# Five modulation vectors summed beside the FFN's first product, and its first pair of columns computed by eight plain products

## The chip, the cores and the metric

The kernel runs on one core of a Trainium2 chip. The metric is the device time of one execution in microseconds, the median of three runs. The profile is one further execution, recorded by the hardware profiler.

## The reference, cut to what matters

Two transformer blocks run one after the other on one sequence of 1024 tokens with 1024 channels, all in float32. The part that the change touches is the feed-forward network that ends block 1, and the modulation vectors of both blocks:

```python
mod = c_act @ ada_w[i] + ada_b[i]                 # 6 vectors of 1024 (block 1)
sh1, sc1, g1, sh2, sc2, g2 = split(mod, 6)
...
h = rmsnorm(x, ffn_norm_pre) * (1 + sc2) + sh2
a, b = split(h @ ffn_w_in, 2)                     # 1024 x 5632: two halves of 2816 columns
y = (silu(a) * b) @ ffn_w_out                     # 2816 x 1024
x = x + g2 * rmsnorm(y, ffn_norm_post)
...
mod = cond @ mod_w + mod_b                        # block 2: 6 more vectors, from c_2
```

`c` and `c_2` are one row each, so a modulation vector is a row times a 1024 x 1024 matrix: 4 MB are read for 1024 numbers.

## The kernel before

[...] A product is then three matmuls per tile: high x high, high x low, low x high (`mm3` and `product`, lines 214 to 221 and 660 to 668). `split` (lines 161 to 164) makes the parts: ScalarE (ACT) copies to the high part, VectorE (DVE) subtracts.

**The first product.** The transposed activations `T` (1024 channels x 1024 tokens) are cut into four blocks: "00", "10" (the first 512 tokens, channels 0 to 511 and 512 to 1023), and two for the second 512 tokens. The 2816 column pairs are taken in 22 steps of 128 (`NH = 22`), step j with one unit of 128 columns from each half of `ffn_w_in`. A plain way needs 8 block products a step (2 units x 2 channel halves x 2 token halves). The kernel uses a scheme with sums of blocks that needs 7: `block_sums` (lines 590 to 632) forms the sums `t1` to `t4` of the activations and their parts once; `left_sums` (lines 634 to 648) forms the matching sums of the weights for every step. `first_two(j)` computes the two products that need no sum (`a11` x "00" and `a12` x "10"), `pair(j)` the other five; each product is 12 matmuls of 512 columns. `prep(j)` loads the two units of a step (512 KB each, tile `raw`, three buffers) and makes the split and the sums. In the loop over j, `prep(j + 1)` is advanced by one step after each product of `pair(j)`.

Before the loop three steps are begun early (`EARLY = 3`): their upper units are split, and their first two products run while the norm of the residual (`norms`) and the block sums are still being computed, mostly on DVE. `prep(0)` follows the block sums, for its sums are written to `SP`, which takes the place of the activations `Y`. The results go to DRAM (`midh`, `midl`).

**The second product** runs in three passes over the 2816 rows of `ffn_w_out` (units 0 to 7, 8 to 15, 16 to 21), each pass over eight row tiles of 128 tokens. For each row tile `load_mid` loads `mth` and `mtl` back, two row tiles ahead.

**The modulation vectors** `G2`, `A3`, `B3`, `Gm`, `A4`, `B4`, `Ge` are computed by `mod_steps` (lines 239 to 270) beside passes 0 and 1: for each vector eight loads of 512 KB into `raw` and eight DVE operations (lines 250 and 252) that add a block of 128 matrix rows, scaled by `cc`, to `acc`; then matmuls with ones sum over the partitions (line 256), DVE adds the bias and the gain from `quad` tiles, and a store writes the vector to DRAM. `mods` is advanced five steps after each row tile.

**The order of the work.** The source issues everything in one sequence, with generators advanced at chosen places. A planner in the kernel framework then fixes the order on each engine and queue at build time: source order is the priority, and an instruction goes ahead of an earlier one where its operands and buffers are there first by the planner's own costs. Buffers of one tag (`raw` 3, `wh` 3, `wl` 3, `k2` 4, `h2` 8, `k4` 8) are handed out as they come free. All loads and stores of this part go through SyncE's queue (SP). Products take PSUM buffers by `pany`, alternating between two sets of three.

Of the kernel before, what the change touches and what calls it, by code (L numbers as in the profile page):

```python
# [10 lines left out]
F32 = mybir.dt.float32  # L11
F32R = mybir.dt.float32r
I32 = mybir.dt.int32
AF = mybir.ActivationFunctionType
OP = mybir.AluOpType
# [4 lines left out]
D = 1024  # L20
# [15 lines left out]
class Kernel:  # L36
# [199 lines left out]
        for g in groups:  # L236
            yield from self.mod_steps(*g)

    def mod_steps(self, m, cc, vectors):


        nc, a = self.nc, self.a
        w, b = a[m + "_w" + self.suffix[m]], a[m + "_b" + self.suffix[m]]
        for name, j, g in vectors:
            acc = self.k4([128, D], "acc")
            for k in range(8):
                raw = self.wp.tile([128, 1024], F32, name="raw", bufs=self.raw_bufs)
                nc.sync.dma_start(raw, w[0, k * 128:(k + 1) * 128, j * D:(j + 1) * D])
                if k == 0:
                    nc.vector.tensor_scalar(acc, raw, cc[:, 0:1], None, op0=OP.mult)  # L250
                else:
                    nc.vector.scalar_tensor_tensor(acc, raw, cc[:, k:k + 1], acc, op0=OP.mult, op1=OP.add)  # L252
                yield
            ps = self.pany()
            for q in range(4):
                nc.tensor.matmul(ps[32 * q:32 * q + 32, 0:256], self.one[:, 0:32], acc[:, q * 256:(q + 1) * 256],
                                 start=True, stop=True, tile_position=(0, 32 * q))

            def quad(v):
                t = self.k2([128, 256], "quad")  # L260
                nc.sync.dma_start(t, bass.AP(tensor=v.tensor, offset=v.offset, ap=[[256, 4], [0, 32], [1, 256]]))
                return t

            t = self.k2([128, 256], "quad")
            nc.vector.tensor_tensor(t, ps[:, 0:256], quad(b[0, j * D:(j + 1) * D]), op=OP.add)
            if g is not None:
                nc.vector.scalar_tensor_tensor(t, t, g[0], quad(a[g[1]]), op0=OP.add, op1=OP.mult)
            d = self.r[name] = self.dram.tile([1, D], F32, name="r" + name)
            nc.sync.dma_start(d.rearrange("o (q n) -> (o q) n", q=4), t[0:128:32, :])
# [400 lines left out]
    def block1_ffn(self, dbg=None):  # L670
        nc, tc, a = self.nc, self.tc, self.a
        V = nc.vector
        TH, TL, Y = self.TH, self.TL, self.Y
        w_in, w_out = a["ffn_w_in"], a["ffn_w_out"]
        NH = 22
# [18 lines left out]
        src = lambda j: [w_in[0, :, c:c + 128].rearrange("(k p) m -> p k m", p=128) for c in (j * 128, (NH + j) * 128)]  # L694
        W, TT = {}, {}

        def upper(j, raw):
            W[j] = [self.wp.tile([128, 1024], F32R, name=n, bufs=self.hl_bufs) for n in ("wh", "wl")]
            self.split(W[j][0], W[j][1], raw)

        def prep(j, lone):

            raw = [self.raw_unit(u, (8, 128)) for u in src(j)]
            if not lone:
                upper(j, raw[0])
            yield
            W[j] += [self.k2([128, 512], n, F32R) for n in ("a22h", "a22l")] + [SP[:, j % 2 * 4 + n] for n in range(4)]
            yield from self.left_sums(raw, W[j][2:4], W[j][4:])

        def first_two(j):  # L710

            A, T = self.left_parts(W[j]), self.T
            TT[j] = t = {}
            ps = self.pany()
            self.product(ps, A["a11"], T["00"])
            t[0] = self.h2([128, 512], "p1")
            nc.scalar.activation(t[0], ps, AF.Copy)
            yield
            ps = self.pany()
            self.product(ps, A["a12"], T["10"])  # L720
            t[2] = self.h2([128, 512], "sa")
            V.tensor_tensor(t[2], ps, t[0], op=OP.add)
            nc.scalar.activation(t[2], t[2], AF.Silu)

        def out(j, half, m):
            s = slice(half * 512, half * 512 + 512)
            h, l = self.h2([128, 512], "mh", F32R), self.h2([128, 512], "ml", F32R)
            self.split(h, l, m)
            for d, t in zip(midd, (h, l)):
                nc.sync.dma_start(d[j, :, s], f32(t))  # L730
# [29 lines left out]
            out(j, 1, t[3])  # L760
            del W[j], TT[j]

        EARLY = 3
        for j in range(EARLY):
            upper(j, self.raw_unit(src(j)[0], (8, 128)))
        self.T = {"00": ([TH[:, k, 0:512] for k in range(4)], [TL[:, k, 0:512] for k in range(4)]),
                  "10": ([TH[:, 4 + k, 0:512] for k in range(4)], [TL[:, 4 + k, 0:512] for k in range(4)])}
        early = [first_two(j) for j in range(EARLY)]
        for _ in norms:
            next(early[0], None)  # L770
        for f in early[:2]:
            for _ in f:
                pass
        for k, _ in enumerate(self.block_sums(B2)):
            if k == 1:
                for _ in early[2]:
                    pass
        SP = self.region(1, "SP", F32R)
        for _ in prep(0, True):
            pass  # L780
        for j in range(NH):
            nxt = prep(j + 1, j + 1 < EARLY) if j + 1 < NH else iter(())
            for _ in pair(j, j < EARLY):
                next(nxt, None)
            for _ in nxt:
                pass


        cc2 = self.silu_col(a["c_2"], "cc2")
        mods = self.all_mods(("ada", self.cc, (("G2", 5, (0.0, "ffn_norm_post")),)),  # L790
                             ("mod", cc2, (("A3", 1, (1.0, "norm1_g_2")), ("B3", 0, None), ("Gm", 2, None),
                                           ("A4", 4, (1.0, "norm2_g_2")), ("B4", 3, None), ("Ge", 5, None))))
        wide = lambda f: [f([128, 1024], n, F32R) for n in ("oh", "ol")]
        wpt = lambda: [self.wp.tile([128, 1024], F32R, name=n, bufs=self.hl_bufs) for n in ("wh", "wl")]
        U = {}
# [24 lines left out]
        for at, (c, i) in enumerate(todo):  # L820
            last = c == 2
            if (c, i) == (1, 6):
                for _ in mods:
                    pass
            if (c, i) == (1, 7):
                G2, A3 = self.bcast(self.r["G2"], "G2"), self.bcast(self.r["A3"], "A3")
                B3 = self.load_cols(self.const, self.r["B3"], "B3")
                self.cw = self.load_cols(self.const, a["conv_w_2"], "cw", 32)
                self.cbias = self.load_cols(self.const, a["conv_b_2"], "cvb", 8)
            mt = mts.pop((c, i))  # L830
            pss = [self.pany(), self.pany()]

            order = passes[c] if c else [0, 1, 2, 3, 4, 5, 6, 7]
            for n, j in enumerate(order):
                u = j - passes[c][0]
                for nh in range(2):
                    q = slice(nh * 512, nh * 512 + 512)
                    h, l = U[j][0][:, q], U[j][1][:, q]
                    nc.tensor.matmul(pss[nh], mt[0][:, u], h, start=n == 0, stop=False)
                    nc.tensor.matmul(pss[nh], mt[0][:, u], l, start=False, stop=False)  # L840
                    nc.tensor.matmul(pss[nh], mt[1][:, u], h, start=False, stop=n == len(order) - 1)
            for nh in range(2):
                q = slice(nh * 512, nh * 512 + 512)
                if c == 0:
                    nc.scalar.activation(Y[:, i, q], pss[nh], AF.Copy)
                else:
                    V.tensor_tensor(Y[:, i, q], Y[:, i, q], pss[nh], op=OP.add)
            if at + 2 < len(todo):
                load_mid(*todo[at + 2])

            if c == 0 and i in (3, 4, 5):
                unit(8 + i - 3, (OH[:, 5 + i - 3], OL[:, 5 + i - 3]))
            if c == 0 and i == 7:
                for j in range(11, 16):
                    unit(j, (OH[:, j - 11], OL[:, j - 11]))
            if c == 1 and i < 6:
                unit(16 + i, wpt() if i < 3 else wide(self.k4))
            if c < 2:
                for _ in range(5):
                    next(mods, None)  # L860
            else:
                if i == 0:
                    TH, TL = self.TH, self.TL = self.region(2, "TH", F32R), self.region(3, "TL", F32R)
                    norms = self.norms(lambda i: self.residual_norm(
                        i, G2, A3, x1[rows(i), :], self.x2[rows(i), :], self.xt_slot(i, True)))
                next(norms)
                if i == 6:
                    self.half_to_T(0, B3)
# [1073 lines left out]
```

## Time and profile before

| | |
|---|---|
| timed runs | 2839.19, 2839.96, 2842.51 us; median 2839.96 |
| profiled execution | 2849.81 us, span 2848.1 us from first to last instruction |
| busy over the span | PE 92%, weight loads 74%, DVE 62%, ACT 44%, POOL 8% |
| moved by DMA | 443 MB, mean 156 GB/s |

The profile's page names engines as PE (TensorE matmuls), PEld (weight loads), DVE, ACT, POOL and SP, and lines as L252. A share of busy time over the whole span averages stages with different limits, so the stretches around the change are read one by one: the start of the first product (about 485 to 513 us), its loop (513 to 922 us), passes 0 and 1 of the second product (922 to 1144 us).

### The profile page before, as it was taken

Reading aid. Unit: us, or ns where it says so; the run is one execution under the profiler, and the core shown is the slowest. Engines: PE = TensorE matmul, PEld = TensorE weight load, DVE = VectorE, ACT = ScalarE, POOL = GpSimd, SP = SyncE. Lnnn points to the kernel's source line nnn. Section 1 sums busy time; section 2 is a strip of 40 time slices with the busy share of each in tenths; the row PEclk is TensorE's granted clock in tenths of the full one; section 3 lists DMA queues with packets and bytes.
Section 4 is the critical chain, followed back from the end, with each engine's and each line's share of the span. In section 5 each row is a group of like instructions: output and inputs, shape, how many; then the busy total and the mean of one; then the engine's idle time right before and its main releaser. Section 6 shows DMA issues by size and latency. Waiting matters only on the chain. (4 is left out here: it accounts for less than half of the span.)

```text
span 2848.1 us, 36415 instructions
## 1 busy us (share of the span) xinstructions
PE 2631.1 (92%) x13146; PEld 2117.0 (74%) x13146; DVE 1777.7 (62%) x3672; ACT 1252.6 (44%) x2184; POOL 215.2 (8%) x204
## 2 busy tenths in 40 slices
PE   6999997899999989899999999999999999798882
PEld 4766675688887767778988888788887878677772
DVE  6666549877676454676510444547777468788885
ACT  4666645333333110144321333334555444677782
POOL 0000011000000000100000000000000200333320
PEclk9999999899999999999999999999999999899996
DMA  7233122332334887434434554551111454799995
GB/s 242 89 97 97 36 89 97 118 119 96 111 118 155 275 272 245 133 115 151 139 111 103 181 163 142 176 189 39 30 31 40 155 199 146 249 331 327 311 327 181
DMA packets 318828, 443.17 MB, mean 156 GB/s; under 512 B 41665, under 2 KB 215806, under 8 KB 318646
## 3 DMA queue, kind: packets, MB, share of 16 engines
q1 hardware_dynamic: 309430, 424.02, 45.2%
q0 software_dynamic: 9216, 16.81, 2.5%
q8 instruction: 104, 1.70, 0.3%
q14 instruction: 78, 0.64, 0.1%
HBM read 355.44 MB, written 102.06 MB: 161 GB/s over the span
## 5 line engine op out<-in xcount | busy, mean ns | idle before, releaser
L164 DVE TENSOR_TENSOR wl<-raw,wh 128x1024 fp32r<-128x1024 f32 (+3 forms) x106 | 130.7, 1233 | 246.7 <-ACT wh L163 236.2
L163 ACT ACTIVATE wh<-raw 128x1024 fp32r<-128x1024 f32 (+3 forms) x106 | 110.4, 1043 | 277.9 <-PE pss L220 134.6
L164 DVE TENSOR_TENSOR mgl<-X,MH 128x1024 fp32r<-128x1024 f32 x91 | 110.1, 1221 | 16.0 <-ACT MH L163 15.4
L252 DVE SCALAR_TENSOR_TENSOR acc<-raw,cc,acc 128x1024 f32<-128x1024 f32 x70 | 89.8, 1283 | 43.1 <-DMA raw<-in_mod_w_dram 35.8
L163 ACT ACTIVATE MH<-X 128x1024 fp32r<-128x1024 f32 x91 | 96.2, 1060 | 38.1 <-DMA X<-in_w_expert_up_dram 16.5
L1744 PEld LDWEIGHTS pss<-mgl,xh 128*128 128x128 f32 x512 | 96.4, 188 | 22.1
L221 PE MATMUL pss<-TH,wl 128*128 128x512 f32 x280 | 111.4, 398 | 0.0
L219 PE MATMUL pss<-TH,wh 128*128 128x512 f32 x280 | 111.1, 397 | 0.0
L220 PE MATMUL pss<-TL,wh 128*128 128x512 f32 x280 | 110.9, 396 | 0.0
L1744 PE MATMUL pss<-mgl,xh 128*128 128x256 f32 x512 | 102.6, 281 | 0.0
L1742 PE MATMUL pss<-MH,xh 128*128 128x512 f32 x256 | 102.5, 400 | 0.0
L1745 PE MATMUL pss<-MH,xl 128*128 128x512 f32 x256 | 101.0, 394 | 0.0
L440 DVE CUSTOM_DVE_ANT_0 pp<-pss,bias 128x384 f32<-128x384 f32 (+1 forms) x128 | 63.4, 521 | 54.4 <-PE pss L436 53.5
L549 POOL TENSOR_TENSOR Y<-Y,G 128x1024 f32<-128x1024 f32 x16 | 39.5, 2467 | 743.5 <-DMA xt<-in_x_dram 412.7
L219 PE MATMUL mm<-TH,wh 128*128 128x512 f32 x232 | 93.1, 401 | 2.4 <-ACT TH L175 1.3
L220 PE MATMUL mm<-TL,wh 128*128 128x512 f32 x232 | 92.3, 398 | 0.0
L221 PE MATMUL mm<-TH,wl 128*128 128x512 f32 x232 | 92.3, 398 | 0.0
L228 PE MATMUL mm<-TH,wh 128*128 128x512 f32 x192 | 78.0, 407 | 1.6 <-ACT TH L348 1.6
L447 ACT ACTIVATE pp<-pp,mx 128x384 f32<-128x384 f32 (+1 forms) x128 | 73.8, 579 | 11.6 <-DVE mx L443 11.6
L219 PE MATMUL mm<-WD,mTh 128*128 128x512 f32 x128 | 55.3, 432 | 24.9 <-ACT mTh L163 24.8
L229 PE MATMUL mm<-TL,wh 128*128 128x512 f32 x192 | 77.5, 404 | 0.6 <-DVE TL L349 0.6
L230 PE MATMUL mm<-TH,wl 128*128 128x512 f32 x192 | 76.6, 399 | 0.0
(732 smaller groups left out, 8154.7 us busy)
## 6 DMA issues: line engine op xcount, KB each, us to landing
raw<-in_mod_w_dram SPq DMA_DIRECT2D x48, 512.0 KB
raw<-in_ffn_w_in_dram SPq DMA_DIRECT2D x47, 512.0 KB
X<-in_w_expert_gate_dram SPq DMA_DIRECT2D x47, 512.0 KB
X<-in_w_expert_down_dram SPq DMA_DIRECT2D x47, 512.0 KB
X<-in_w_expert_up_dram SPq DMA_DIRECT2D x44, 512.0 KB
raw<-in_w_in_dram SPq DMA_DIRECT2D x40, 512.0 KB
raw<-in_ada_w_dram SPq DMA_DIRECT2D x32, 512.0 KB
midh<-mh SPq DMA_DIRECT2D x44, 256.0 KB
```

Of the source, the lines that this page charges most:

```text
L163: self.nc.scalar.activation(h, src, AF.Copy)
L164: (engine or self.nc.vector).tensor_tensor(l, src, f32(h), op=OP.subtract)
L219: nc.tensor.matmul(ps, ah, bh, start=i == 0, stop=False)
L220: nc.tensor.matmul(ps, ah, bl, start=False, stop=False)
L221: nc.tensor.matmul(ps, al, bh, start=False, stop=i == n - 1)
L228: nc.tensor.matmul(ps, ah, bh, start=i == 0, stop=False)
L229: nc.tensor.matmul(ps, ah, bl, start=False, stop=False)
L230: nc.tensor.matmul(ps, al, bh, start=False, stop=i == n - 1)
L252: nc.vector.scalar_tensor_tensor(acc, raw, cc[:, k:k + 1], acc, op0=OP.mult, op1=OP.add)
L1742: nc.tensor.matmul(ps, xh[:, k], gh, start=k == 0, stop=False)
L1744: nc.tensor.matmul(ps[:, c], xh[:, k], self.ML[n + c][:, m], start=False, stop=False)
L1745: nc.tensor.matmul(ps, xl[:, k], gh, start=False, stop=k == 7)
```

## The change

Five of the seven vectors (`G2`, `A3`, `B3`, `Gm`, `A4`) are advanced inside the loop over pairs, three steps in each pair from j = 2 on; `B4` and `Ge` stay beside passes 0 and 1, now two steps after each row tile. `late=3` puts three empty steps between a vector's last DVE operation and its matmuls. For the five, `acc` takes a buffer of the tag `wl` instead of `k4`. The start of the first product: step 0 is computed by eight plain products, four (`usual_first`) beside the norms and four (`usual_second`) after the block sums; only step 1 is begun early by its first two products, and the loop starts at j = 1.

```diff
-    def mod_steps(self, m, cc, vectors):
+    def mod_steps(self, m, cc, vectors, late=0, wl=False):
...
-            acc = self.k4([128, D], "acc")
+            acc = self.wp.tile([128, D], F32, name="acc", tag="wl", bufs=self.hl_bufs) if wl else self.k4([128, D], "acc")
...
+                yield
+            for _ in range(late):
                 yield
             ps = self.pany()
...
-        EARLY = 3
-        for j in range(EARLY):
-            upper(j, self.raw_unit(src(j)[0], (8, 128)))
+        C = []
+        for u in src(0):
+            C += [self.wp.tile([128, 1024], F32R, name=n, bufs=self.hl_bufs) for n in ("wh", "wl")]
+            self.split(C[-2], C[-1], self.raw_unit(u, (8, 128)))
+        upper(1, self.raw_unit(src(1)[0], (8, 128)))
...
-        early = [first_two(j) for j in range(EARLY)]
+        parts = [self.left_parts(C[0:2]), self.left_parts(C[2:4])]
+        kept = []
+
+        def usual_first():
+            for n, A in enumerate(parts):
+                ps = self.pany()
+                self.product(ps, A["a11"], self.T["00"])
+                p = self.h2([128, 512], "p1")
+                nc.scalar.activation(p, ps, AF.Copy)
+                yield
+                ps = self.pany()
+                self.product(ps, A["a12"], self.T["10"])
+                t = self.h2([128, 512], "c1")
+                V.tensor_tensor(t, ps, p, op=OP.add)
+                kept.extend((p, t))
+                if n == 0:
+                    nc.scalar.activation(t, t, AF.Silu)
+                    yield
+            V.tensor_tensor(t, t, kept[1], op=OP.mult)
+            out(0, 0, t)
+
+        def usual_second():
+            for A, p in zip(parts, (kept[0], kept[2])):
+                ps = self.pany()
+                self.mm3(ps, [(A[x][0][k], A[x][1][k], self.T[y][0][k], self.T[y][1][k])
+                              for x, y in (("a11", "t1"), ("a12", "11")) for k in range(4)])
+                V.tensor_tensor(p, ps, p, op=OP.add)
+                if p is kept[0]:
+                    nc.scalar.activation(p, p, AF.Silu)
+            V.tensor_tensor(p, p, kept[0], op=OP.mult)
+            out(0, 1, p)
+
+        f = usual_first()
         for _ in norms:
-            next(early[0], None)
-        for f in early[:2]:
-            for _ in f:
-                pass
+            next(f, None)
+        for _ in f:
+            pass
+        f = first_two(1)
         for k, _ in enumerate(self.block_sums(B2)):
-            if k == 1:
-                for _ in early[2]:
-                    pass
+            next(f, None)
+        usual_second()
         SP = self.region(1, "SP", F32R)
-        for _ in prep(0, True):
+        for _ in prep(1, True):
             pass
-        for j in range(NH):
-            nxt = prep(j + 1, j + 1 < EARLY) if j + 1 < NH else iter(())
-            for _ in pair(j, j < EARLY):
+        cc2 = self.silu_col(a["c_2"], "cc2")
+        mods = self.all_mods(("ada", self.cc, (("G2", 5, (0.0, "ffn_norm_post")),), 3, True),
+                             ("mod", cc2, (("A3", 1, (1.0, "norm1_g_2")), ("B3", 0, None), ("Gm", 2, None),
+                                           ("A4", 4, (1.0, "norm2_g_2"))), 3, True))
+        for j in range(1, NH):
+            nxt = prep(j + 1, False) if j + 1 < NH else iter(())
+            for n, _ in enumerate(pair(j, j == 1)):
                 next(nxt, None)
+                if j > 1 and n in (0, 2, 4):
+                    next(mods, None)
             for _ in nxt:
                 pass
-        cc2 = self.silu_col(a["c_2"], "cc2")
-        mods = self.all_mods(...)
+        for _ in mods:
+            pass
+        mods = self.all_mods(("mod", cc2, (("B4", 3, None), ("Ge", 5, None)), 3))
...
             if c < 2:
-                for _ in range(5):
+                for _ in range(2):
                     next(mods, None)
```

## Rows read from the trace of the kernel before

**Rows 1.** The page's 40 slices, tenths: granted clock of PE, share of DMA.
```profile
PEclk9999999899999999999999999999999999899996
DMA  7233122332334887434434554551111454799995
```

**Rows 2.** Busy time by stretch; counts in brackets, then granted clock, DMA share, GB/s.
```profile
485.00:513.00 28.00, 10.87 (x53) 8.20 (x52) 25.53 (x39) 14.16 (x23) 0.00 (x0) 0.70 0.07 21
...
620.00:776.00 156.00, 156.00 (x675) 126.42 (x674) 110.67 (x152) 54.64 (x72) 0.00 (x0) 1.00 0.33 109
922.00:1144.00 222.00, 195.22 (x829) 149.72 (x829) 106.27 (x108) 30.66 (x39) 0.00 (x0) 0.94 0.83 260
```

**Rows 3.** Timeline of one pair in the loop: start, duration, engine, line, operation.
```profile
598.21 0.38 SPq L189 DMA_DIRECT2D raw<-in_ffn_w_in_dram  x1
...
602.31 1.06 ACT L163 ACTIVATE wh<-raw 128x1024 fp32r<-128x1024 f32 x1 [2.86 <-PE pss L668]
...
607.64 0.63 ACT L163 ACTIVATE a22h<-raw 128x512 fp32r<-128x512 f32 x1 [4.27 <-PE pss L667]
...
616.43 1.23 DVE L164 TENSOR_TENSOR SP<-raw,SP 128x1024 fp32r<-128x1024 f32 x1 [0.40 <-ACT SP L163]
...
617.68 0.39 SPq L189 DMA_DIRECT2D raw<-in_ffn_w_in_dram  x1
...
635.50 0.40 PE L666 MATMUL mm<-t2h,SP 128*128 128x512 f32 x1
```

**Rows 4.** Waits of PE, 922 to 1144 us: total, times, longest.
```profile
PE mm L256 <- DVE acc L252: 11.1, 3, 4.8
PE pss L256 <- DVE acc L252: 8.6, 1, 8.6
...
PE pss L839 <- DMA mth<-midh: 2.0, 1, 2.0
```

**Rows 5.** Timeline of PE behind the longest of these waits.
```profile
1059.50 0.63 PE L840 MATMUL pss<-OL,mth 128*128 128x512 f32 x1
...
1062.84 0.39 PE L840 MATMUL pss<-OL,mth 128*128 128x512 f32 x1
```

**Rows 6.** Busy time by stretch, start of the second product.
```profile
920.00:930.00 10.00, 8.35 (x36) 6.02 (x34) 6.72 (x9) 4.69 (x7) 0.34 (x1) 1.00 1.02 305
930.00:940.00 10.00, 8.84 (x31) 6.91 (x32) 4.49 (x4) 2.11 (x2) 0.00 (x0) 0.83 0.84 276
```

**Rows 7.** Timeline of PE: a vector's eight matmuls beside the attention.
```profile
165.61 0.64 PE L256 MATMUL mm<-acc,one 128*32 128x256 f32 x8
```

**Rows 8.** The page's costliest groups: busy us, mean ns, idle before and releaser.
```profile
L252 DVE SCALAR_TENSOR_TENSOR acc<-raw,cc,acc 128x1024 f32<-128x1024 f32 x70 | 89.8, 1283 | 43.1 <-DMA raw<-in_mod_w_dram 35.8
```

**Rows 9.** Waits of DVE in the loop, 620 to 776 us.
```profile
DVE p L741 <- PE pss L668: 10.1, 12, 1.4
...
DVE u L741 <- PE pss L668: 8.2, 4, 2.1
DVE wl L164 <- ACT wh L163: 4.3, 8, 0.8
DVE SP L164 <- ACT SP L163: 3.2, 8, 0.4
```

**Rows 10.** Timeline of the stop at the start of the first product.
```profile
503.57 0.75 DVE L630 SCALAR_TENSOR_TENSOR TL<-pss,B,TH 128x512 fp32r<-128x512 f32 x1
...
508.17 0.80 PE L666 MATMUL mm<-TH,SP 128*128 128x512 f32 x1 [13.43 <-ACT SP L163]
...
512.71 0.39 PE L666 MATMUL pss<-t2h,SP 128*128 128x512 f32 x1
```

**Rows 11.** Waits of DVE on loads, 922 to 1144 us.
```profile
DVE acc L252 <- DMA raw<-in_mod_w_dram: 35.8, 26, 5.0
...
DVE acc L252 <- DMA raw<-in_ada_w_dram: 6.8, 4, 2.9
```

More of the change, by code (lines that the diff above doesn't have):

```diff
@@ L784, in block1_ffn @@
                 next(nxt, None)
+                if j > 1 and n in (0, 2, 4):
+                    next(mods, None)
             for _ in nxt:
                 pass
-        cc2 = self.silu_col(a["c_2"], "cc2")
-        mods = self.all_mods(("ada", self.cc, (("G2", 5, (0.0, "ffn_norm_post")),)),
-                             ("mod", cc2, (("A3", 1, (1.0, "norm1_g_2")), ("B3", 0, None), ("Gm", 2, None),
-                                           ("A4", 4, (1.0, "norm2_g_2")), ("B4", 3, None), ("Ge", 5, None))))
+        for _ in mods:
+            pass
```

## The prediction

> **What bounds the kernel now.** I read the 40 slices first: where DMA stands at nine tenths while PEclk dips, TensorE waits for transfers; where both are calm it computes [rows 1]. The second view, busy time by stretch, splits the part around the change into three stages [rows 2]. In the loop over column pairs (620 to 776 us) PE is busy without a gap at full clock, 156.00 of 156.00 us, VectorE (DVE) is busy 110.67 us and the DMA share is 0.33: TensorE bounds it. In passes 0 and 1 of the second product (922 to 1144 us) PE is busy 195.22 of 222.00 us, the clock is 0.94 and the DMA share 0.83. At the start of the first product (485 to 513 us) PE is busy 10.87 of 28.00 us and DVE 25.53: DVE bounds it.
>
> The pitch of a 512-column product comes from the loop: a load of `raw` is issued 19.47 us after its like of the pair before [rows 3], and a pair has 7 products of 12 matmuls, so 19.47 / 84 = 0.232 us, or 2.78 us a product. Passes 0 and 1 hold 2 passes x 8 row tiles x 8 units x 2 halves x 3 = 768 matmuls, 178.0 us. They took 222, so 44 us are lost there. [...] The start of the stage costs 4.5 us: 36 + 31 matmuls in 20 us where 86 would fit [rows 6]. That start waits for units of `ffn_w_out`, not for vectors, and stays.
>
> **The change, part by part.**
>
> *Passes 0 and 1 lose five of seven vectors.* Forty loads of 512 KB go, 21.0 MB of the 260 GB/s x 222 us = 57.7 MB [rows 2]. What is left, 36.7 MB, asks for some 196 GB/s over 187 us, three quarters of what the stage carries now. The two vectors left get two steps per row tile instead of five and their PE part comes three steps after the last sum, 1.5 row tiles or 16 us later; the longest wait for a sum was 8.6 us [rows 4]. So I count all four waits and the slow clock behind them as gone. After: 178.0 for the products, 2 x 0.64 = 1.3 for the vectors' own matmuls (eight in 0.64 us [rows 7]), 4.5 for the start, and something for waits that remain on `mth`, `mtl` and units. That last term lies between 0 (nothing late) and what today's loss leaves: 44.0 - 7 x 0.64 for seven vectors' matmuls - 4.5 for the start - 19.7 = 15.3 us, which is the clock lost behind the four waits and the waits on transfers. Of the second sort the row shows 2.0 us on `mth` [rows 4]; I take 3.5, near it, with something for the clock, since row tile 7 of pass 0 still asks for five units at once. Sum 187.3, a gain of 34.7 us; its bounds are 38.2 and 22.9.
>
> *The pair loop gets them.* PE: 5 x 0.64 = +3.2 us, for PE has no gap there to hide it. DVE: 40 operations on `acc` of 1.283 us [rows 8], 51 us, and eight short ones on a quarter of the columns, 0.32 each by an estimate from that width: 54 us, less a little because the first of each vector has one operand fewer; 52 over the 18.3 pairs that 55 steps need at three a pair, 2.84 us a pair. DVE now works 110.67 / 8 = 13.83 us a pair [rows 2] and waits 36.0 us in eight pairs for PE itself (four rows, from 10.1 to 8.2 [rows 9]), 4.5 a pair. The addition fits into the wait for PE and leaves 1.66 us a pair. It hides because evictions may lag: six PSUM buffers at 2.78 us a product. If that cover were gone, all 52 us would show. SP: 40 loads, 5 + 3 rows of bias and gain, 5 stores and one row of `c_2` at some 0.38 us of issue each [rows 3] are 21 us on a queue that issues six transfers a pair. Behind them in that queue stand the next pair's loads and the stores of `mh`/`ml`; POOL's queue is untouched.
>
> *Buffers.* A pair's two loads hold two of the three `raw` buffers; forty vector loads pass through what is free, 2.2 a pair. Vector data taken late delays the next pair's left sums. Those have room: issued at 598.21, split from 607.64, done by 617.7, first used at 635.50 [rows 3], some 18 us of slack. `acc` now takes one of three `wl` buffers, so upper weights can be split only one pair ahead, which is all that PE needs. The five `quad` tails take slots that `a22h`/`a22l` use and can hold them for two loads and a store, 12 us at most if each takes the 4.1 us from a load's issue to its first use (598.21 to 602.31 [rows 3]): inside the 18 us, and if it were not, PE would wait for the excess, five times. For all of this I take +1 us, with 0 below and rival C on the other side. The row of `c_2` and its transpose are put ahead of the loop: 0 to 3 us, counted in that 1.
>
> *The first pair by eight products.* Before the stop PE has six products in either version (3 x 2 before, 4 + 2 after). The stop: PE waits 13.43 us for `SP`, to 508.17, and then runs at the lower level until 512.7 [rows 10]. After it stand 3 x 5 + 19 x 7 = 148 products before, and 4 + 5 + 20 x 7 = 149 after. But the first four of those, 11.1 us, need only `t1` and `11`, whose last low part is written at 503.57 to 504.3 [rows 10], so they run inside the stop, and 145 stand behind it: 3 x 2.78 = 8.3 us less. Against that, DVE, the bound here, gets one multiplication and one low part more ahead of the block sums and four such operations beside the left sums, each some 0.75 as line 630 [rows 10], so `SP` comes 1.5 to 4.5 us later. The clock lost after the stop (508.17 to 512.71 at half pace, 2.3 us) is partly saved. I take a gain of 6 us; bounds 10 (all in the stop, most of the clock kept) and -2.8 (nothing hidden, one product more).
>
> *Sum.* -34.7 + 3.2 + 1 - 6 = -36.5 us. The profiled execution is 2849.8 us (span 2848.1 and 1.7 around it), so 2813.3 by its own time. The three timed runs have a median of 2840.0, 0.35% lower; the same difference gives 2803.5, rounded 2804.
>
> **Rivals.**
>
> B. The second product stays bound by its own transfers. For it: share 0.83 now, and rows show waits on `mth` and units that are no vector's. Against: 196 GB/s is asked where 260 is carried. Then all of the 15.3 us stays: -22.9 + 4.2 - 6 = -24.7, 2815. Its cost above that would be loads that come later than today, for which no row speaks.
>
> C, on the other side: DVE becomes the bound of the pair loop. Its order is fixed when the kernel is built; a sum whose load is late holds back every eviction and left sum behind it. Place: pairs 2 to 19. Point: 1.66 us a pair, 30 us over 18 pairs, is 0.75 us for each of 40 loads; beyond that each microsecond of mean wait costs 40, and at 1.66 us the whole gain is eaten. In the second product the sums waited 42.6 us in 30 cases, 1.42 each, 0.76 over all 56 loads, the longest 5.0 [rows 11]. With half the longest, 2.5: 40 x 1.75 = +70, 2873. Against: that was at a DMA share of 0.83; here it goes from 0.33 (109 GB/s) to some 0.5 by 60 GB/s more, and 42.6 of the 43.1 us that this line was idle in the whole kernel [rows 8] lie in the second product: next to none beside the attention, where three vectors are summed through the same three buffers.
> [...]
>
> D. The eight-product start gains nothing: one product more and the added DVE work shift everything, +2.8 instead of -6: 2813. For it: DVE is busy 25.53 of 28 us there. Against: the four products need no left sums.
>
> E. The change doesn't do what it says: the planner leaves the vectors' loads behind the pairs' own until the loop ends, and the drain there costs what the stage saved: about 2838. Against: three steps a pair stand in the source order, and buffers come free twice a pair.
>
> **Chances.** Forecast 0.60, B 0.15, C 0.10, D 0.10, E 0.05. The likeliest case alone lies in 2795 to 2813 (-38.2 + 3.2 - 10 = -45; -31 + 4.2 + 0 = -26.8). For 8 in 10 I take 2791 to 2833: the forecast's own range with 4 us below (the timed runs differ by 3.3), B, D and the mild end of C (mean wait 1.42 us: +27, 2831); E and most of C lie outside. A measurement here tells 0.2%, 5.7 us, from no change. Faster by more: forecast, B, D, 0.85. Within: E, 0.05. Slower: C, 0.10.
>
> **What would show it.** In the profile after: PE without a gap through the pair loop, DVE near 16.7 us a pair, DMA share near 0.5; passes 0 and 1 in 184 to 191 us with no wait of line 256 on line 252; PE busy between 495 and 508 with `TH`/`wl` products of the first pair. DVE above 19 us a pair including waits on `raw`, or PE waiting for `SP` inside the loop, shows C. `mth` waits above 7 us show B. A stop before the first `SP` product of more than 5 us shows D. The prediction is wrong above all if loads inside the loop come later than the left sums' 18 us of slack.

## The result, and the profile after

The kernel after takes 2808.64 us (median of four runs, 2806.95 to 2810.86) against 2841.24 for the kernel before (median of four, the three known before among them): ratio 0.9884, 95% interval 0.9867 to 0.9901, or 32.6 us faster. The forecast was 2804 in 2791 to 2833. The profiled execution, one of these four, took 2807.7 us where the sum said 2813.3.

Busy time by stretch of the kernel after; columns as in [rows 2]:
```profile
485.00:513.00 28.00, 22.25 (x97) 17.10 (x96) 27.82 (x43) 15.98 (x26) 0.00 (x0) 0.88 0.02 6
620.00:776.00 156.00, 156.00 (x684) 125.37 (x683) 131.64 (x174) 53.51 (x72) 0.00 (x0) 1.00 0.54 173
918.00:1103.60 185.60, 182.30 (x787) 145.72 (x788) 55.13 (x60) 30.52 (x38) 0.00 (x0) 0.99 0.62 193
```
Beside [rows 2], PE is busy for twice as long at the start; in the loop it still has no gap, while DVE's busy time rises from 110.67 to 131.64 us, 16.5 a pair; passes 0 and 1 take 185.6 us where they took 222, at a DMA share of 0.62 instead of 0.83.

All waits of PE in passes 0 and 1 after (total, times, longest):
```profile
PE pss L880 <- ACT OH L163: 3.4, 2, 2.2
```
The waits for sums of [rows 4] are gone, and the one row left is the start of the stage. Line 880 is the old 839; 668 to 670 are the old 666 to 668, 743 and 753 evictions (VectorE takes a finished product out of its PSUM buffer), 258 the old 256.

PE at the start of the first product, after:
```profile
490.84 0.77 PE L609 MATMUL pt<-ident,Y 128*128 128x128 f32 x4 [2.37 <-ACT x L621]
...
501.62 0.79 PE L219 MATMUL pss<-TH,wh 128*128 128x512 f32 x1 [3.37 <-ACT TH L163]
...
510.61 0.50 PE L668 MATMUL mm<-TH,SP 128*128 128x512 f32 x1
```
The wait of 13.43 us for `SP` [rows 10] has become one of 3.37 us for a part of `t1`; from there the plain products of step 0 run, and `SP` is no longer waited for.

DVE in the loop, 530 to 900 us, the waits that stand before or in a sum's chain:
```profile
DVE acc L252 <- DMA raw<-in_mod_w_dram: 17.8, 18, 2.2
DVE wl L164 <- ACT wh L163: 7.9, 9, 2.5
...
DVE acc L252 <- DMA raw<-in_ada_w_dram: 1.7, 4, 0.6
...
DVE acc L250 <- DMA raw<-in_ada_w_dram: 0.9, 1, 0.9
```
Sums do wait for their loads, 20.4 us over 40 loads, 0.51 each, and PE doesn't notice.

To compare kernels by stage I use three starts of every trace: the first matmul of the second half of the attention's output projection (about 401 us), the first of pass 0 and the first of pass 2. Lengths in us, worked out from these starts (a second profile of before and of after are the runs e0 and a1):

| kernel | to pass 0 | passes 0, 1 | timed median, ratio to before |
|---|---|---|---|
| before / e0 | 521.56 / 521.56 | 220.96 / 219.73 | |
| after / a1 | 518.36 / 518.68 | 184.51 / 184.39 | 2808.64, 0.9884 / 2806.06, 0.9867 |
| e1 start alone | 514.17 | 216.50 | 2835.74, 0.9977 |
| e2 vectors alone | 525.26 | 184.61 | 2813.55, 0.9900 |
| e3 empty steps alone | 521.70 | 206.16 | 2832.58, 0.9963 |
| e4 seven vectors, four steps | 528.83 | 181.90 | 2819.20, 0.9916 |
| e5 more DVE work | 518.31 | 184.63 | 2807.08, 0.9872 |
| e8 four steps | 526.45 | 184.13 | 2811.86, 0.9892 |
| e9 no empty steps | 524.75 | 182.44 | 2815.59, 0.9895 |
| e6 order of pass 0 | 517.09 | 183.03 | 2805.61, 0.9868 |
| e7 norm on DVE | 507.48 | 184.78 | 2792.87, 0.9823 |
| e10 both | 506.01 | 182.83 | 2790.97, 0.9819 |

The median of before lay between 2843.39 and 2844.64 us in the comparisons with e1 to e10.

### The profile page after: what moved, and what is told of

Its sections match the earlier page's. It is cut to its first block, busy times and chain, and to the rows that moved or that the text cites. A ratio compares the mean times of both kernels' runs of the same rounds, so it can differ in the third digit from the quotient of the medians.

```text
span 2805.8 us, 36372 instructions
## 1 busy us (share of the span) xinstructions
PE 2627.1 (94%) x13158; PEld 2116.6 (75%) x13158; DVE 1765.9 (63%) x3663; ACT 1249.7 (45%) x2183; POOL 219.3 (8%) x204
## 5 line engine op out<-in xcount | busy, mean ns | idle before, releaser
L164 DVE TENSOR_TENSOR wl<-raw,wh 128x1024 fp32r<-128x1024 f32 (+2 forms) x107 | 132.9, 1242 | 243.7 <-ACT wh L163 233.0
L163 ACT ACTIVATE wh<-raw 128x1024 fp32r<-128x1024 f32 (+2 forms) x107 | 111.5, 1043 | 238.2 <-PE mm L220 142.1
L164 DVE TENSOR_TENSOR mgl<-X,MH 128x1024 fp32r<-128x1024 f32 x91 | 110.0, 1221 | 16.5 <-ACT MH L163 16.0
L221 PE MATMUL mm<-TH,wl 128*128 128x512 f32 x288 | 114.6, 398 | 0.0
L219 PE MATMUL mm<-TH,wh 128*128 128x512 f32 x288 | 114.5, 397 | 0.0
L220 PE MATMUL mm<-TL,wh 128*128 128x512 f32 x288 | 114.2, 396 | 0.0
L163 ACT ACTIVATE MH<-X 128x1024 fp32r<-128x1024 f32 x91 | 96.3, 1062 | 37.8 <-DMA X<-in_w_expert_up_dram 15.9
L219 PE MATMUL pss<-TH,wh 128*128 128x512 f32 x240 | 97.8, 408 | 5.7 <-ACT TH L163 4.4
L220 PE MATMUL pss<-TL,wh 128*128 128x512 f32 x240 | 96.6, 403 | 0.0
L221 PE MATMUL pss<-TH,wl 128*128 128x512 f32 x240 | 96.3, 401 | 0.0
L228 PE MATMUL mm<-TH,wh 128*128 128x512 f32 x192 | 78.5, 410 | 1.0 <-ACT TH L350 1.0
L229 PE MATMUL mm<-TL,wh 128*128 128x512 f32 x192 | 77.6, 404 | 0.0
L230 PE MATMUL mm<-TH,wl 128*128 128x512 f32 x192 | 76.6, 399 | 0.0
```

What stands on the lines that cost most here:

```text
L163: self.nc.scalar.activation(h, src, AF.Copy)
L164: (engine or self.nc.vector).tensor_tensor(l, src, f32(h), op=OP.subtract)
L219: nc.tensor.matmul(ps, ah, bh, start=i == 0, stop=False)
L220: nc.tensor.matmul(ps, ah, bl, start=False, stop=False)
L221: nc.tensor.matmul(ps, al, bh, start=False, stop=i == n - 1)
L228: nc.tensor.matmul(ps, ah, bh, start=i == 0, stop=False)
```

## The experiments

**The two parts apart, e1 and e2.**
```diff
 # e1: kernel after, vectors as in the kernel before
-        mods = self.all_mods(("ada", self.cc, (...), 3, True), ("mod", cc2, (...), 3, True))
...
-                if j > 1 and n in (0, 2, 4):
-                    next(mods, None)
...
+        mods = <all seven, behind the loop, five steps a row tile>
 # e2: kernel before, with the lines that e1 takes out added and EARLY = 3 kept
```


> The eight-product start of step 0 alone; all seven vectors stay beside passes 0 and 1, five steps a row tile, no empty steps. Theory T1 (the gain is the sum of two independent parts: passes 0 and 1 relieved of five vectors, and the start's stop filled with four products): the start alone gives 6 to 8 us over the kernel before, 2833 to 2835, and PE's waits for the vectors' sums (line 252) in passes 0 and 1 stay near the 19.7 us of the kernel before. Rival R1 (the start only moves the wait, DVE being the bound there): within 2 us of before. Rival R2 (the start gives all that the forecast missed and more): 10 us or more.

> The five vectors moved beside the first product with their empty steps, but the three early steps of the kernel before at the start. T1: 26 to 31 us faster than before, 2810 to 2815; passes 0 and 1 in 184 to 188 us and the loop longer by 3 to 4 us. Rival R2: 20 us or less. If the two parts need each other (the start leaves fewer upper units in the buffers that the sums now share), this one is slower than T1 says by the waits on wl buffers in the first pairs: 5 to 10 us.

e1: ratio 0.9977 (0.9968 to 0.9986), by the ratio 6.5 us. e2: 0.9900 (0.9883 to 0.9916), 28.4 us. Together 34.9, against 32.6 measured for both at once: within the intervals the parts are independent, as T1 says, and R1, R2 and the coupling through `wl` fall. The stages show more than the times: the start alone shortens the way to pass 0 by 7.4 us, the vectors lengthen it by 3.70 (e2 against before) or 4.19 (after against e1), and passes 0 and 1 take 184.6 us with the vectors' move alone. In e1, whose profiled execution lies at its timed median (2835.37 against 2835.74), these passes take 216.5 us with all seven vectors in them. Measured from there the move gives 31.9 us and costs 3.7, 28.2 in all, as e2's time says; measured from the profile of before it would be 36.4 - 3.7 = 32.7.

Waits of PE in passes 0 and 1 of e1:
```profile
PE pss L258 <- DVE acc L252: 10.3, 3, 4.4
PE mm L258 <- DVE acc L252: 9.7, 3, 8.1
```
20.0 us of waits for sums, as in [rows 4]. The stop of e2, which keeps the old start:
```profile
502.89 0.24 PE L133 MATMUL pt<-ident,crow 8*128 8x8 f32 x1 [8.68 <-DMA crow<-in_c_dram]
507.64 0.80 PE L668 MATMUL mm<-TH,SP 128*128 128x512 f32 x1 [4.52 <-ACT SP L163]
```
The transpose of `c_2`'s row is queued inside the stop and costs nothing there: 8.68 + 4.52 are 13.2 us, and before waited 13.43.

**The empty steps alone, e3.**
```diff
 # kernel before
-        ("ada", self.cc, (("G2", ...),)), ("mod", cc2, (...))
+        ("ada", self.cc, (("G2", ...),), 3), ("mod", cc2, (...), 3)
...
-                for _ in range(5):
+                for _ in range(6):
```


> All seven vectors stay beside passes 0 and 1 and only PE's part of each is put three steps later (six steps a row tile, so that the loads keep about their pace). Rival R3 (PE's waits for the sums are the loss, so the empty steps alone recover it): the 19.7 us of waits and the slow clock behind them go, 20 to 28 us faster than before. T1 (the transfers of 58 MB in this stage are the loss; a wait for a sum is where it shows): 12 us faster at most, with the DMA share still above 0.8 and waits of PE on mth, mtl or units in the place of those on sums.

Ratio 0.9963 (0.9950 to 0.9976), 10.5 us. R3 falls: putting PE's part later recovers 10.5 of the 28.4 us that e2's move gives, and part of that may come from the loads, which run at 4.4 a row tile here (6 steps, 8 loads in 11) instead of 5. Waits of PE in e3, 900 to 1145 us (its line 841 is the old 839), and the first wait of DVE, 922.8 to 1129 us:
```profile
PE mm L258 <- DVE acc L252: 5.7, 2, 3.6
PE mm L841 <- DMA mth<-midh: 3.3, 1, 3.3
PE pss L258 <- DVE acc L252: 3.0, 3, 1.5
```
```profile
DVE acc L252 <- DMA raw<-in_mod_w_dram: 32.2, 23, 3.5
```
8.7 us of waits for sums remain, a wait of 3.3 us on `mth` stands beside them (2.0 in [rows 4]), and the sums themselves still wait for their loads, at a DMA share of 0.86 in this stage: late loads are behind the loss, and a later place for PE's part only moves where that is felt. Whether the rate of the transfers or their issue through three `raw` buffers makes them late, no run tells apart: in the kernel before the queue stands 34.9 us until a sum frees a buffer for the next vector load (922 to 1144 us).

**What VectorE bears in the loop, e5.**
```diff
                     nc.vector.scalar_tensor_tensor(acc, raw, cc[:, k:k + 1], acc, op0=OP.mult, op1=OP.add)
+                if wl:
+                    nc.vector.tensor_tensor(raw, raw, raw, op=OP.max)
```


> The kernel after with one more VectorE operation behind each of the 40 additions of a vector in the loop (the maximum of a raw tile with itself, in place, 128 x 1024; 1.22 us like line 164 of that shape; the tile's buffer is held that much longer). 40 x 1.22 = 49 us over 18.3 pairs, 2.7 us a pair: DVE 16.5 + 2.7 = 19.2 of a 19.47 us pair, and with the mean wait for raw (0.51 us x 2.2 loads a pair = 1.1) 20.3. Theory C1 (in the loop VectorE's busy time and its waits for raw add up against the pair, and only the excess shows): 0.8 us x 18 pairs, some 15 us slower than after, 2820 to 2828, with stops of PE on evictions. Rival C2 (the waits are swallowed by the slack of the evictions): within 3 us of after. Rival C3 (any delay of VectorE shows in full): 45 us or more slower.

2807.08 us, ratio 0.9872 (0.9856 to 0.9888), and 518.31 us to pass 0 against 518.36: nothing. C1 and C3 fall. Busy time of e5 in the loop, and two of its DVE waits, 530 to 900 us:
```profile
620.00:776.00 156.00, 156.00 (x685) 125.29 (x684) 148.29 (x191) 53.48 (x72) 0.00 (x0) 1.00 0.52 168
```
```profile
DVE acc L252 <- DMA raw<-in_mod_w_dram: 2.5, 6, 0.9
...
DVE wl L164 <- ACT wh L163: 2.1, 2, 1.3
```
DVE is busy 148.29 of 156 us, 95%, and PE has no gap. The waits for `raw` fell from 20.4 to 3.6 us (2.5 + 0.7 + 0.4): the added operations run where DVE had stood waiting. Busy time and waits don't add up, so the 1.66 us a pair of the prediction was no limit.

**The pace of the loads, e4, e8 and e9.**
```diff
 # e4: all seven vectors in the loop; e8: the five of the change; both:
-                if j > 1 and n in (0, 2, 4):
+                if j > 1 and n in (0, 1, 2, 4):
 # e9: kernel after
-        (..., 3, True) ... (..., 3)
+        (..., 0, True) ... (..., 0)
```


> The kernel after with all seven vectors beside the first product, four steps a pair in place of three; nothing is left beside passes 0 and 1. T1: the loop pays 2 x 0.64 = 1.3 us more of PE, DVE goes from 16.5 to some 17.4 us of a 19.5 us pair and still hides; passes 0 and 1 lose the 1.3 us of PE that move: the same time as the kernel after within 2 us, 2807 to 2811. Rival C (DVE with its late loads is near the bound of the loop): the 56 sums wait more, pairs stretch past 19.6 us, 8 us or more slower than after.

> The kernel after, its five vectors at four steps a pair in place of three: the same 40 loads and sums, done in 14 pairs instead of 18. It tells whether the 8 us that seven vectors at four steps lost come from the pace (theory C1: 2.9 sums a pair, a stop of PE inside the loop of 6 us as there, some 5 to 10 us slower than after) or from the two vectors more and their work at the loop's end (rival: within 2 us of after, no stop of PE inside the loop).

> The kernel after without the three empty steps, in the loop and in passes 0 and 1: PE's eight matmuls of a vector follow its last sum in the source order, as in the kernel before. Theory D1 (sums in the loop are seldom late, so the move itself is nearly the whole gain and the empty steps only insure it): within 3 us of after, with PE's waits for line 252 below 3 us in total. Rival D2 (the move needs the empty steps: in the loop PE has no gap, so each of five vectors stops it for the sum's own 1.28 us and the lateness of its load, up to 3 us, and the clock drops behind it): 10 to 20 us slower than after.

e4: ratio 0.9916 (0.9902 to 0.9930), 2819.20 us, some 10 slower than after: rival C's outcome. e8: 0.9892 (0.9875 to 0.9908); its time can't be told from that of after, but the way to pass 0 is 8.1 us longer, most of e4's 10.5. So the two vectors more are not the reason. PE and then DVE at the stop of e8:
```profile
701.67 0.39 PE L670 MATMUL pss<-TH,SP 128*128 128x512 f32 x1
707.35 0.80 PE L668 MATMUL mm<-TH,wh 128*128 128x512 f32 x1 [5.29 <-DVE c L753]
707.94 0.63 PE L669 MATMUL mm<-TL,wh 128*128 128x512 f32 x1
```
```profile
700.16 1.29 DVE L252 SCALAR_TENSOR_TENSOR acc<-raw,cc,acc 128x1024 f32<-128x1024 f32 x1 [1.87 <-DMA raw<-in_mod_w_dram]
701.36 0.68 DVE L743 TENSOR_TENSOR u<-mm,p 128x512 f32<-128x512 f32 x1
702.66 1.22 DVE L164 TENSOR_TENSOR wl<-raw,wh 128x1024 fp32r<-128x1024 f32 x1 [0.62 <-ACT wh L163]
703.81 0.68 DVE L743 TENSOR_TENSOR p<-pss,p 128x512 f32<-128x512 f32 x1
705.41 1.28 DVE L252 SCALAR_TENSOR_TENSOR acc<-raw,cc,acc 128x1024 f32<-128x1024 f32 x1 [0.92 <-DMA raw<-in_mod_w_dram]
706.61 0.69 DVE L753 TENSOR_TENSOR c<-mm,p 128x512 f32<-128x512 f32 x1
```
This is the mechanism of rival C, of which the rows of before held no case. The eviction `c` stands in DVE's queue behind two sums that wait 1.87 and 0.92 us for their loads and a low part that waits 0.62 us for its split. PE waits 5.29 us until `c`, which reads an `mm` buffer, has run; then its matmuls take 0.63 us instead of 0.39 to 0.40. Between 620 and 776 us, the stretch of this stop, DVE was *less* busy than in e5:
```profile
620.00:776.00 156.00, 150.71 (x653) 120.00 (x652) 127.54 (x169) 51.07 (x69) 0.00 (x0) 0.98 0.56 177
```
Nor do the sums of e8 wait longer: 15.9 us from 530 to 900 us (12.4 + 2.8 + 0.7), where the kernel after has 20.4. What counts is what stands behind a late sum. And it is one stop: e8 has no other in its 14 pairs at this pace, and e4 loses 6.13 us at the same place of the same order (308.4 us after the start that all traces share, e8 306.6) and 0.58 at one other.

e9 was meant to test the empty steps as cover for PE's part. It missed that question: PE never waits for line 252 in its loop. But without them five vectors take 40 steps in place of 55, so the loads run at 3 a pair instead of 2.2, as e8's at 2.9 (40 loads over 55 / 4 pairs). Waits of PE, then of DVE, in the loop of e9, 530 to 900 us:
```profile
PE mm L668 <- DVE c L753: 2.9, 2, 1.6
PE pss L668 <- DVE c L753: 1.5, 2, 1.2
PE pss L668 <- DVE p L743: 0.9, 1, 0.9
```
```profile
DVE wl L164 <- ACT wh L163: 20.5, 14, 3.9
DVE acc L252 <- DMA raw<-in_mod_w_dram: 18.1, 20, 2.1
```
Again PE waits for evictions, 5.3 us in all, and the time is 2815.59 us where after took 2806.06 beside it (ratios 0.9895, 0.9879 to 0.9912, and 0.9867, 0.9851 to 0.9884). The intervals overlap, and two of e9's six runs took 2806.59 and 2810.48 us, as the kernel after does: the loss does not come in every run. DVE waits 20.5 us for the pair's own upper weights, 7.9 in the kernel after. That the vectors' loads have taken the `raw` buffers that these need is likely but not shown: loads of weights stand in the queue until a sum frees a buffer for 12.4 us in e9 and 14.4 in the kernel after. What e4, e8 and e9 have in common is 2.9 to 3 loads a pair. Whether the three buffers or the planner's order of DVE's queue makes that too many was not tried; the single stops of e4 and e8 speak for the order.

**The start of the second product, e6.**
```diff
-            order = passes[c] if c else [0, 1, 2, 3, 4, 5, 6, 7]
+            order = passes[c] if c else [5, 6, 7, 0, 1, 2, 3, 4]
```


> The kernel after, with pass 0 taking its units in the order 5, 6, 7, 0 to 4 (5 to 7 lie in wh/wl, loaded during the last pairs; 0 to 4 go to the places of the activations, which come free when the loop ends). Theory: the two waits of PE for OH at the start of the second product (1.15 and 2.21 us) and the slow clock behind the second one are hidden behind 36 matmuls of the first two row tiles: 3 to 4.5 us faster than after. Rival (the loads of units 0 to 4 come later by as much, for they wait for raw buffers): within 1.5 us of after, with the waits moved to the second row tile.

Waits of PE in passes 0 and 1 of e6:
```profile
PE pss L881 <- DVE OL L164: 0.8, 1, 0.8
PE pss L880 <- ACT OH L163: 0.6, 1, 0.6
PE pss L882 <- DMA mtl<-midl: 0.5, 1, 0.5
```
3.4 us of waits become 1.9, and the two stages together are 2.75 us shorter than after's. The time (0.9868, 0.9852 to 0.9885) can't be told from that of after.

**Before again, e0** (no edit).

> The kernel before once more, for a second profile: the first profiled execution took 2849.8 us where the timed ones lie near 2841. If the 8 us lie in passes 0 and 1 (theory: the waits for late transfers vary from run to run), this stage takes 213 to 217 us here instead of 221, and all others are the same within 1.5 us; if they lie elsewhere, the stage is 220 to 222 again.

Missed: the stage took 219.7 us again, and the execution 2848.83, above the seven timed runs beside it (2840.32 to 2845.85). e1, with all seven vectors in that stage, took 216.5. That points to passes 0 and 1 for 3 to 4.5 of the 4 to 9 us that the profiled executions of before lose against the timed ones; where the rest lies stays open, for no profile of before fell near its median.

**The norms, e7, e10 and a1.** The traces showed a cost that the change does not touch. VectorE operations on 128 x 1 values in the residual norm, after:
```profile
413.17 2.41 POOL L551 TENSOR_TENSOR Y<-Y,G 128x1024 f32<-128x1024 f32 x1 [411.77 <-ACT junk L159]
...
413.31 0.15 DVE L107 TENSOR_SCALAR rs<-ms 128x1 int32<-128x1 int32 x1
413.50 2.10 DVE L113 SCALAR_TENSOR_TENSOR rt<-rs,ms 128x1 f32<-128x1 f32 x1
415.62 0.15 DVE L119 TENSOR_SCALAR ru<-rt 128x1 f32<-128x1 f32 x1
...
416.41 2.39 POOL L551 TENSOR_TENSOR Y<-Y,G 128x1024 f32<-128x1024 f32 x1 [0.84 <-ACT junk L159]
...
416.65 2.18 DVE L124 TENSOR_TENSOR rs<-rs,rt 128x1 f32<-128x1 f32 x1
```
The operations of lines 113 and 124 end with GpSimd's (at 415.60 and 418.83 against 415.58 and 418.80). Line 107, with one tensor as input, runs in 0.15 us while GpSimd's runs. Whether GpSimd's work is what holds them up is tested by giving it to VectorE:
```diff
-        nc.gpsimd.tensor_tensor(Yi, Yi, G, op=OP.mult)
+        nc.vector.tensor_tensor(Yi, Yi, G, op=OP.mult)
 # e10: this and e6's order; a1: kernel after, unchanged
```


> The kernel after with the multiplication of a row tile by the gain in the residual norm (16 of 128 x 1024) on VectorE in place of GpSimd. In the trace some VectorE operations on 128 x 1 values take 2.0 to 2.2 us in place of 0.15 to 0.22 while GpSimd works on such a tile, at most one or two per tile. Theory N1 (these 2 us, 7 or so in each of the two stages with norms, are VectorE held up by GpSimd, and VectorE bounds these stages): 14 x 2.0 us go, 16 x 1.22 us are added, and the pairs of norms no longer wait for a product of 2.46 us: 3 to 10 us faster than after. Rival N2 (VectorE's own 1.22 us a tile cost as much): within 3 us of after or slower.

> The kernel after with both: units 5 to 7 first in pass 0, and the gain's multiplication on VectorE. If the two are independent, it is 3 us faster than the run with the multiplication alone, and 3 us plus that run's gain faster than after.

> The kernel after once more, beside the three others on the same chip: 2806 to 2810, and the start of passes 0 and 1 within 2 us of the first profile.

e7: 2792.87 us, ratio 0.9823 (0.9809 to 0.9837), 13.2 us faster than after's 2806.06 beside it: N1, and more than its 10 at most. The same groups of DVE, 400 to 490 us, after and e7 (busy us, mean ns, idle before):
```profile
L113 DVE SCALAR_TENSOR_TENSOR rt<-rs,ms 128x1 f32<-128x1 f32 x32 | 12.2, 380 | 0.7
...
L120 DVE TENSOR_TENSOR ru<-ru,rt 128x1 f32<-128x1 f32 x16 | 8.6, 536 | 0.4
...
L124 DVE TENSOR_TENSOR rs<-rs,rt 128x1 f32<-128x1 f32 x16 | 5.3, 328 | 0.3
```
```profile
L551 DVE TENSOR_TENSOR Y<-Y,G 128x1024 f32<-128x1024 f32 x8 | 9.8, 1220 | 4.1 <-ACT junk L159 4.1
...
L113 DVE SCALAR_TENSOR_TENSOR rt<-rs,ms 128x1 f32<-128x1 f32 x32 | 5.7, 214 | 0.1
...
L124 DVE TENSOR_TENSOR rs<-rs,rt 128x1 f32<-128x1 f32 x16 | 2.3, 156 | 0.1
L120 DVE TENSOR_TENSOR ru<-ru,rt 128x1 f32<-128x1 f32 x16 | 2.3, 156 | 0.1
```
9.8 us are added and 15.8 saved in these groups. The stretch from the first of the three starts to the first matmul that reads `SP`, after and e7:
```profile
400.74:510.61 109.87, 93.82 (x410) 73.77 (x410) 98.60 (x224) 56.34 (x90) 19.70 (x8) 0.91 0.34 124
```
```profile
403.55:502.54 98.99, 90.89 (x410) 71.62 (x410) 89.42 (x232) 56.24 (x90) 0.00 (x0) 0.93 0.39 137
```
For the same 410 matmuls e7 takes 10.9 us less, and DVE, the busiest engine here, is busy 9.2 us less although it has eight operations more. So most of the gain is VectorE's own time, as N1 says; that a tile's chain no longer runs through an operation of 2.46 us on another engine can account for the other 1.7 us at most. The way to pass 0 is 11.2 us shorter than a1's, which repeats the kernel after as expected (2806.06 us, both stages within 0.4 us of the first profile). e10 takes 2790.97 us, 0.9819 (0.9805 to 0.9833): the fastest of all, 15.1 us below after beside it. Its 1.9 us below e7 lie within the spread of the runs; by the stages it is 3.4.

## Why the prediction was right, step by step

- **Passes 0 and 1** (predicted 222.0 to 187.3, a gain of 34.7): 222.0 to 185.6, or 36.4 to 36.5 by the profiles of the two kernels, and 32.0 against e1's 216.5, the likelier figure for the timed runs. The matmuls, 178.0, and the two vectors' 1.3 stand; the start of the stage keeps its waits (3.4 us) and a slow stretch behind the second (granted clock 0.50 from 928.13 to 931.51 us), 6.3 us where the sum had 4.5. The 19.7 us of the sum are the four waits of [rows 4]. The slow clock behind them stands in [rows 5] for the longest: the granted clock was 0.50 from 1058 to 1060 us and 1.00 from 1062.84 to 1070 us. The 3.5 us that I left for other waits were not needed: no wait on `mth`, `mtl` or `acc`. Rival B falls with that, and e3 shows why the move was needed: late loads bound the stage, not the place of PE's part.
- **Loop** (+3.2 and +1): 3.70 and 4.19 us by the two pairs of kernels that differ in it.
- **Start** (-6): 7.4 us by the stages, 6.5 by e1's time. The lower level behind the stop of [rows 10] was a granted clock of 0.50 from 508.17 to 512.71 us, and 1.00 from there to 520 us. Rival D falls: DVE was the bound there, but four products needed nothing that it made late.
- **Rival C** had the right mechanism and place, with the wrong point and price. I set the point where DVE's busy time and waits fill the pair (1.66 us a pair). e5 put 49 us of DVE work into the loop and the waits shrank. It came up at 2.9 to 3 loads a pair instead, where an eviction stood behind a late sum, and cost one to five stops of PE of 0.3 to 6 us, 6 to 8 us of the way to pass 0 for five vectors, not 40 us for each microsecond of mean wait. The change stays clear of it at 2.2 loads a pair, in part through its empty steps.
- **Rival E** falls: DVE's work is spread over the loop, 16.5 us a pair as predicted.
- **The conversion to the timed median** was the weak step. By profiled executions the gain is 42.1 us, 5.6 more than the sum's 36.5: 1.7 in passes 0 and 1, 1.4 at the start and 2.5 in parts of the kernel that the change does not touch, where profiles of one kernel differ by as much. But I scaled the sum by the ratio of before's own profile to its median (9.8 us), and the profile of after does not lie above its median: 2807.7 against 2808.6. The two errors, +5.6 and -10.7 (9.8, and the 0.9 from profile to median), leave the 5.1 us by which 2803.5 misses; that they partly cancel is luck.
- **One reading of [rows 1]** was wrong, and nothing in the sum rests on it: the slices at nine tenths of DMA keep a granted clock of 9, and the dips of the clock stand at 3, 7 and 5 tenths.

## What to carry to other kernels

Move traffic out of a stage that transfers bind into one that TensorE bounds, and count the loads per step of the receiving loop against the buffers that they share with its own loads: here 2.2 a step cost no stop, and 2.9 to 3 cost 6 to 8 us, most of it in single stops, whatever VectorE's busy share said. Then look in the trace at what stands behind each late sum. In e5 a busy share of 95% on VectorE cost nothing (518.31 us to pass 0 against 518.36); in e8, at 82% (127.54 of 156 us), an eviction behind two sums that waited 1.87 and 0.92 us for their loads stopped PE for 5.29 us. Before a sum worked out from one profiled execution is scaled to the timed median, see from a second profile whether that one was typical.

## What the runs showed of the hardware that was not expected

In the kernel after, two-input VectorE operations on 128 x 1 values took 2.0 to 2.2 us instead of 0.16 to 0.22 beside 14 of GpSimd's 16 multiplications of a 128 x 1024 tile; beside the other two they took 1.79 and 0.84 us. Giving GpSimd's 16 multiplications (2.46 us each) to VectorE (1.22 each) made the kernel 13.2 us faster, although VectorE was already busy 98.60 of 109.87 us in the first of the two stages with norms.
